# RMSNorm with doubled rows: squares by the whole tile, issued one tile ahead on ScalarE, and nearly all the copies on ScalarE

**Chip, cores, metric.** One core of a Trainium2 chip. The metric is the device time of one execution in microseconds (us); the span of the profiled execution is about 2 us shorter. All runs quoted are at a granted clock of 1.0.

## The reference

```python
B, S, D = 8, 512, 2048                      # float32
x_rep  = np.repeat(x, 2, axis=1)            # each row twice
rms    = np.sqrt((x_rep ** 2).mean(axis=-1, keepdims=True) + 1e-6)
out    = (x_rep / rms) * gamma              # [8, 1024, 2048]
```

33.6 MB are read and 67.1 MB written.

## The kernel before

Eight tiles. A tile is 128 partitions by 4 rows of 2048; its buffer has 8 row slots. The load fills slots 4 to 7, the scaled rows go to slots 0, 2, 4, 6, their copies to 1, 3, 5, 7, and one store writes all eight. There are three buffers, so load i+3 waits until store i has landed. All loads and stores go through SyncE, in program order.

```python
def square(i, k):                           # ScalarE: row squares into PSUM, with their sum
    sq = junk.tile([P, D], f32, name="sq")
    nc.scalar.activation(out=sq[:], in_=ys[i][:, 4 + k, :], func=Act.Square, accum_out=ss[:])
    nc.scalar.activation(out=rms[:], in_=ss[:], func=Act.Sqrt, scale=inv_d, bias=eps_t[:])
    ...
def scale(i, k, rms):                       # VectorE
    nc.vector.reciprocal(out=rstd[:], in_=rms[:])
    nc.vector.scalar_tensor_tensor(out=ys[i][:, 2 * k, :], in0=ys[i][:, 4 + k, :], scalar=rstd[:],
                                   in1=gamma_b[:], op0=Alu.mult, op1=Alu.mult)
def compute(i):
    for k in range(4):
        scale(i, k, square(i, k))
    repeat(i, 0, 2, nc.scalar.copy)         # copies of rows 0, 1
    repeat(i, 2, 4, nc.vector.tensor_copy)  # copies of rows 2, 3
...
load(0), load(1), load(2)
loads_after = {2: (3, 4, 5), 4: (6, 7)}
for i in range(8):
    compute(i)
    store(i, 0, 4)
    for j in loads_after.get(i, ()):
        load(j, nc.sync)
```

(Slot numbers are written out here; tile declarations and the load of gamma are cut.)

## Time and profile before

| | before |
|---|---|
| time, median | 239.9 us (239.40 to 240.17, 5 runs) |
| span of the profile | 237.9 us |
| instructions | 287 |
| VectorE busy | 96.5 us |
| ScalarE busy | 101.0 us |
| SyncE's queue, share of 16 engines' span | 98.5% |

The last row is the one to start from: the queue moves data during nearly the whole span, while both compute engines rest for over half of it. The lines that show this stand in the prediction. A store may be issued at any moment before the transfers queued ahead of it are over, less the time that it takes to start; only after that does lateness cost time.

A transfer is cut into packets, which 16 DMA engines move side by side. The trace records each packet's start, length, size and queue, but not its engine; where the text speaks of one engine, packets were chained, each to the one that ended as it began.

### The profile page before, as it was taken

Reading aid. Unit: us, or ns where it says so; the run is one execution under the profiler, and the core shown is the slowest. Engines: PE = TensorE matmul, PEld = TensorE weight load, DVE = VectorE, ACT = ScalarE, POOL = GpSimd, SP = SyncE. Lnnn points to the kernel's source line nnn. Section 1 sums busy time; section 2 is a strip of 40 time slices with the busy share of each in tenths; the row PEclk is TensorE's granted clock in tenths of the full one; section 3 lists DMA queues with packets and bytes.
Section 4 is the critical chain, followed back from the end, with each engine's and each line's share of the span. In section 5 each row is a group of like instructions: output and inputs, shape, how many; then the busy total and the mean of one; then the engine's idle time right before and its main releaser. Section 6 shows DMA issues by size and latency. Waiting matters only on the chain.

```text
span 237.9 us, 287 instructions
## 1 busy us (share of the span) xinstructions
DVE 96.5 (41%) x73; ACT 101.0 (42%) x106; POOL 2.5 (1%) x5
## 2 busy tenths in 40 slices
DVE  0049999960000000059999960000199990000000
ACT  2697999900000000099999920000599960000000
POOL 0030000000000000000000000000000000000000
DMA  7999998989899998999998999989998989999994
GB/s 265 436 446 441 441 441 353 530 353 496 386 452 430 397 485 353 441 441 441 441 518 364 464 419 430 452 369 430 435 518 364 518 364 485 397 452 430 408 474 176
DMA packets 2464, 100.69 MB, mean 423 GB/s; under 512 B 279, under 2 KB 285, under 8 KB 286
## 3 DMA queue, kind: packets, MB, share of 16 engines
q1 hardware_dynamic: 2448, 100.66, 98.5%
q14 instruction: 2, 0.02, 0.0%
q10 hardware_dynamic: 14, 0.01, 0.0%
HBM read 33.56 MB, written 67.11 MB: 423 GB/s over the span
## 4 chain that ended last, share of the span: by engine, by line
DMA 58%; ACT 12%; DVE 9%; issue 1%; POOLq 1%; ACTq 1%; SPq 0%
DMA y<-in_x_dram 33%; DMA out_dram<-y 21%; ACT sq L64 8%; DVE y L74 7%; DMA gamma_b<-in_gamma_dram 4%; ACT y L81 3%; DVE y L81 2%; ACT rms L68 1%; POOLq L136 1%; ACTq L95 1%; DVE rstd L73 0%; POOLq L96 0%; SPq L56 0%
## 5 line engine op out<-in xcount | busy, mean ns | idle before, releaser
L64 ACT ACTIVATE sq<-y 128x2048 f32<-128x2048 f32 x32 | 59.7, 1865 | 87.8 <-DMA y<-in_x_dram 87.8
L74 DVE SCALAR_TENSOR_TENSOR y<-y,rstd,gamma_b 128x2048 f32<-128x2048 f32 x32 | 75.3, 2352 | 4.1 <-POOL gamma_b L96 3.0
L73 DVE RECIPROCAL rstd<-rms 128x1 f32<-128x1 f32 x32 | 5.0, 158 | 94.6 <-ACT rms L68 94.3
L81 ACT COPY y<-y 128x4096 f32<-128x4096 f32 x8 | 28.7, 3590 | 1.4 <-DVE y L74 1.4
L81 DVE COPY y<-y 128x4096 f32<-128x4096 f32 x8 | 18.3, 2294 | 0.3
L68 ACT ACTIVATE rms<-ss,eps_t 128x1 f32<-128x1 f32 x32 | 9.4, 295 | 1.0
L64 ACT ACTIVATION_READ_ACCUMULATOR sq<-y 128x1 f32 x32 | 6.0, 187 | 0.0
L64 ACT ACT_TABLE_LOAD x1 | 1.3, 1283 | 3.0 <-issue 3.0
L96 POOL PARTITION_BROADCAST gamma_b<-gamma_b x1 | 2.3, 2294 | 12.2 <-DMA y<-in_x_dram 12.2
L68 ACT ACT_TABLE_LOAD x1 | 1.3, 1283 | 0.0
L98 DVE MEMSET eps_t<- 128x1 f32 x1 | 0.1, 59 | 0.8 <-PEq L125 0.8
L125 POOL MEMSET const-uint8-127<- 128x1 uint8 x1 | 0.1, 102 | 0.0
L125 POOL MEMSET const-bfloat16-1.0<- 128x1 bf16 x1 | 0.1, 101 | 0.0
L125 POOL MEMSET const-float32-0.0<- 128x1 f32 x1 | 0.1, 98 | 0.2 <-issue 0.2
L125 POOL MEMSET const-float32-1.0<- 128x1 f32 x1 | 0.1, 98 | 0.0
## 6 DMA issues: line engine op xcount, KB each, us to landing
y<-in_x_dram SPq DMA_DIRECT2D x7, 4096.0 KB, 14.6
y<-in_x_dram SPq DMA_DIRECT2D x2, 2048.0 KB, 7.4
out_dram<-y SPq DMA_DIRECT2D x8, 24.4
gamma_b<-in_gamma_dram ACTq DMA_DIRECT2D x6, 1.0 KB
gamma_b<-in_gamma_dram ACTq DMA_DIRECT2D x1, 2.0 KB
```

Source lines behind the costliest of these rows:

```text
L64: nc.scalar.activation(out=sq[:], in_=ys[i][:, K * (R - 1) + k, :], func=Act.Square, accum_out=ss[:])
L68: nc.scalar.activation(out=rms[:], in_=ss[:], func=Act.Sqrt, scale=inv_d, bias=eps_t[:])
L73: nc.vector.reciprocal(out=rstd[:], in_=rms[:])
L74: nc.vector.scalar_tensor_tensor(out=ys[i][:, R * k, :], in0=ys[i][:, K * (R - 1) + k, :], scalar=rstd[:], in1=gamma_b[:], op0=Alu.mult, o ...
L81: copy(out=y_r[:, k0:k1, 1, :], in_=y_r[:, k0:k1, 0, :])
L95: nc.scalar.dma_start(out=gamma_b[0:1, c0:c1], in_=gamma[c0:c1].partition_broadcast(1))
L96: nc.gpsimd.partition_broadcast(out_ap=gamma_b[:], in_ap=gamma_b[0:1, :])
L98: nc.vector.memset(eps_t, eps)
L125: nc = _bacc.Bacc("TRN2", target_bir_lowering=False, num_devices=1)
L136: with _tile.TileContext(nc) as tc:
```

## The change

The intent is to spend fewer instructions. A tile's squares are made by one ScalarE instruction over 8192 elements instead of four with accumulators, written to the slots of the buffer that are still free, and summed by one VectorE reduce. The wide square of tile i+1 is issued ahead of tile i's copies. Tiles 2, 5, 6 and 7 do this; tiles 0 and 3 still work row by row, and tiles 1 and 4 half and half. The copies, except for half of those of tiles 0 and 3, go to ScalarE. Core of the diff:

```diff
+    def square(i, k0, k1):
+        nc.scalar.activation(out=ys[i][:, k0:k1, :], in_=ys[i][:, 4 + k0 : 4 + k1, :], func=Act.Square)
+    def reduce(i, k0, k1, ss):
+        nc.vector.tensor_reduce(out=ss[:, k0:k1], in_=ys[i][:, k0:k1, :], op=Alu.add, axis=X)
+    def wide_tile(i):                       # the wide square of i was issued earlier
+        reduce(i, 0, K, ss); rsqrt(0, K, ss, rstd); scale(i, 0, K, rstd)
-    for i in range(ntiles):
-        compute(i)
-        store(i, 0, K)
-        for j in loads_after.get(i, ()): load(j, nc.sync)
+    ... (tiles 0 to 4)
+    store(4, 0, K)
+    for j in (6, 7): load(j, nc.sync)
+    for i in (5, 6, 7):
+        wide_tile(i)
+        if i < ntiles - 1:
+            square(i + 1, 0, K)
+        repeat(i, 0, H)                     # both copies on ScalarE, behind the square of i+1
+        repeat(i, H, K)
         store(i, 0, K)
```

(Shortened: slots written out, the row and half versions and tiles 0 to 4 cut.)

More of the change, by code (lines that the diff above doesn't have):

```diff
@@ L59, in store, with total @@
         )
-    def square(i, k):
+    def total(i, k, ss):
         sq = junk.tile([P, D], f32, name="sq")
-        ss = small.tile([P, 1], f32, name="ss")
         nc.scalar.activation(
-            out=sq[:], in_=ys[i][:, K * (R - 1) + k, :], func=Act.Square, accum_out=ss[:]
+            out=sq[:], in_=ys[i][:, K * (R - 1) + k, :], func=Act.Square, accum_out=ss[:, k : k + 1]
         )
-        rms = small.tile([P, 1], f32, name="rms")
-        nc.scalar.activation(out=rms[:], in_=ss[:], func=Act.Sqrt, scale=inv_d, bias=eps_t[:])
-        return rms
@@ L71, in scale @@
-    def scale(i, k, rms):
-        rstd = small.tile([P, 1], f32, name="rstd")
-        nc.vector.reciprocal(out=rstd[:], in_=rms[:])
-        nc.vector.scalar_tensor_tensor(
-            out=ys[i][:, R * k, :], in0=ys[i][:, K * (R - 1) + k, :], scalar=rstd[:], in1=gamma_b[:],
-            op0=Alu.mult, op1=Alu.mult,
-        )
-    def repeat(i, k0, k1, copy):
+    def square(i, k0, k1):
+        x_at = K * (R - 1)
+        nc.scalar.activation(
+            out=ys[i][:, k0:k1, :], in_=ys[i][:, x_at + k0 : x_at + k1, :], func=Act.Square
+        )
@@ new lines, in reduce, with rsqrt, scale @@
+    def reduce(i, k0, k1, ss):
+        nc.vector.tensor_reduce(
+            out=ss[:, k0:k1], in_=ys[i][:, k0:k1, :], op=Alu.add, axis=mybir.AxisListType.X
+        )
+    def rsqrt(k0, k1, ss, rstd):
+        nc.scalar.activation(
+            out=rstd[:, k0:k1], in_=ss[:, k0:k1], func=Act.Sqrt, scale=inv_d, bias=eps_t[:]
+        )
+        nc.vector.reciprocal(out=rstd[:, k0:k1], in_=rstd[:, k0:k1])
+    def scale(i, k0, k1, rstd):
+        for k in range(k0, k1):
+            nc.vector.scalar_tensor_tensor(
+                out=ys[i][:, R * k, :], in0=ys[i][:, K * (R - 1) + k, :], scalar=rstd[:, k : k + 1],
+                in1=gamma_b[:], op0=Alu.mult, op1=Alu.mult,
+            )
@@ L80, in repeat, with columns, rows_tile @@
+    def repeat(i, k0, k1, copy=nc.scalar.copy):
         y_r = ys[i].rearrange("p (k r) d -> p k r d", r=R)
         copy(out=y_r[:, k0:k1, 1, :], in_=y_r[:, k0:k1, 0, :])
-    def compute(i):
-        for k in range(K):
-            scale(i, k, square(i, k))
-        repeat(i, 0, K // 2, nc.scalar.copy)
-        repeat(i, K // 2, K, nc.vector.tensor_copy)
+    H = K // 2
+    def columns():
+        return small.tile([P, K], f32, name="ss"), small.tile([P, K], f32, name="rstd")
+    def rows_tile(i, copy=nc.vector.tensor_copy):
+        ss, rstd = columns()
+        for k0 in (0, H):
+            for k in range(k0, k0 + H):
+                total(i, k, ss)
+            rsqrt(k0, k0 + H, ss, rstd)
+            scale(i, k0, k0 + H, rstd)
+        repeat(i, 0, H)
+        repeat(i, H, K, copy)
@@ L90, with half_tile @@
+    def half_tile(i):
+        ss, rstd = columns()
+        square(i, H, K)
+        for k in range(H):
+            total(i, k, ss)
+        reduce(i, H, K, ss)
+        rsqrt(0, K, ss, rstd)
+        scale(i, 0, K, rstd)
+    def wide_tile(i):
+        ss, rstd = columns()
+        reduce(i, 0, K, ss)
+        rsqrt(0, K, ss, rstd)
+        scale(i, 0, K, rstd)
     ctx.enter_context(tc.manual_schedule())
@@ L104 @@
     assert ntiles == 8
-    loads_after = {2: (3, 4, 5), 4: (6, 7)}
-    for i in range(ntiles):
-        compute(i)
+    rows_tile(0)
+    store(0, 0, K)
+    half_tile(1)
+    square(2, 0, K)
+    repeat(1, 0, H)
+    repeat(1, H, K)
+    store(1, 0, K)
+    wide_tile(2)
+    repeat(2, 0, H)
+    repeat(2, H, K)
+    store(2, 0, K)
+    for j in (3, 4, 5):
+        load(j, nc.sync)
+    rows_tile(3)
+    store(3, 0, K)
+    half_tile(4)
+    square(5, 0, K)
+    repeat(4, 0, H)
+    repeat(4, H, K)
+    store(4, 0, K)
+    for j in (6, 7):
+        load(j, nc.sync)
+    for i in (5, 6, 7):
+        wide_tile(i)
+        if i < ntiles - 1:
+            square(i + 1, 0, K)
+        repeat(i, 0, H)
+        repeat(i, H, K)
         store(i, 0, K)
-        for j in loads_after.get(i, ()):
-            load(j, nc.sync)
 _INS = ['x', 'gamma']
```

## The prediction

> **What bounds the kernel now.** I read the page first. The engines' busy rows, the DMA row and the queue table:
>
> ```profile
> DVE 96.5 (41%) x73; ACT 101.0 (42%) x106; POOL 2.5 (1%) x5
> DMA  7999998989899998999998999989998989999994
> q1 hardware_dynamic: 2448, 100.66, 98.5%
> ```
>
> One queue, SyncE's, moves 100.66 MB and its packets fill 98.5% of the span; VectorE and ScalarE work for 41% and 42% of it. So arithmetic costs time only where it leaves the queue empty. Whether it comes close to that is read from the order of issues on SyncE, in the timeline of that engine (start, length, one issue each; only the second half is needed here):
>
> ```profile
> 91.56 0.33 SPq L52 DMA_DIRECT2D y<-in_x_dram  x1
> 115.86 0.34 SPq L56 DMA_DIRECT2D out_dram<-y  x1
> 128.25 0.34 SPq L56 DMA_DIRECT2D out_dram<-y  x1
> 140.24 0.34 SPq L52 DMA_DIRECT2D y<-in_x_dram  x1
> 159.63 0.34 SPq L52 DMA_DIRECT2D y<-in_x_dram  x1
> 160.08 0.37 SPq L56 DMA_DIRECT2D out_dram<-y  x1
> 184.02 0.34 SPq L56 DMA_DIRECT2D out_dram<-y  x1
> 196.41 0.33 SPq L56 DMA_DIRECT2D out_dram<-y  x1
> ```
>
> These are load 5, stores 3 and 4, loads 6 and 7, stores 5, 6 and 7. The packet records of the trace say when each actually moved: load 5 until 120.6 us, store 3 until 140.2, store 4 until 159.6, load 6 until 169.3, load 7 until 179.3 (its first engine is through at 177.9), then stores 5, 6, 7 back to back until 237.3. A store takes 19.3 us (8 packets of 2.42 us on each engine), a load 9.7 us. There is no gap anywhere after about 3 us: total bytes set the end. Each store therefore has a deadline, the end of what is queued ahead of it, less the start-up of a transfer. Store 5 was issued 19 us before its own. The start-up is seen once on an empty queue: the first load is issued at 0.72 and its packets start between 2.23 and 3.01 us, so 1.5 to 2.3 us.
>
> The chain and ScalarE's timeline show what compute waits for in the last third:
>
> ```profile
> 140.24 29.08 DMA y<-in_x_dram
> 169.32 0.02 issue
> ...
> 169.34 1.88 ACT L64 ACTIVATE sq<-y 128x2048 f32<-128x2048 f32 x1 [30.91 <-DMA y<-in_x_dram]
> ```
>
> Load 6 is issued at 140.24, because its buffer is free only when store 3 has landed, and it lands at 169.3. ScalarE's first square of tile 6 sits 30.91 us waiting for it. That idles nothing that matters today, because tile 5 has been finished since about 140.6 us and its store needs only SyncE.
>
> **What the skill says.** "ScalarE: Activation LUTs", section What ACT_TABLE_LOAD costs: an activation with immediate operands takes 186 ns plus 0.833 ns for each element of a row, and neighbours overlap by some 93 ns. The trace agrees: 3590 ns for the copy of 4096 (3413 + 177), and 3.49 us from its start to that of the next instruction. "VectorE: DVE Perf Modes", section The perf-mode tier table: tensor_reduce has only the 1x mode. This trace has no reduce, so its time is an estimate from that: one element a cycle at 0.96 GHz, 8.53 us for 8192 elements, plus the fixed 0.16 us that the trace's copy has over its 2.13 us. "DMA: Bandwidth & Descriptors", section Anatomy of one DMA: a semaphore wait happens on the issuing sequencer, before dispatch, and the DMA engines just consume their queues. The issue times above agree: the queue runs dry if SyncE is kept waiting. "SBUF — State Buffer", section SBUF: two separate sides: engine and DMA ports cannot contend. The trace agrees: 426 GB/s at 120-140 us, with both engines over 90% busy, and 423 at 200-220 us with both idle; so I charge nothing for the squares that now go to SBUF.
>
> **The change part by part.** Bytes, queue and order of SyncE's issues are unchanged (I compared the instruction orders of both builds). What moves is when each store is ready.
>
> Costs. A wide square: 8192 x 0.833 + 0.18 = 7.0 us, start to next start 6.9; a half one 3.6. 20 of the 32 row squares go (12 stay: 4 each in tiles 0 and 3, 2 each in tiles 1 and 4), 20 x (1.865 + 0.187) = 41.0 us with their accumulator reads, and come back as 4 x 7.0 + 2 x 3.6 = 35.2 us. ScalarE gains six copies of VectorE (6 x 3.59 = 21.5 us) and loses 22 of 32 Sqrt (22 x 0.29 = 6.4). ScalarE: 101.0 - 41.0 + 35.2 + 21.5 - 6.4 = about 110 us. VectorE gains reduces, 4 x 8.7 + 2 x 4.4 = 43.6 us, loses six copies (6 x 2.29 = 13.7) and 22 reciprocals (3.5): about 123 us. Both are half the span still. None of this is on the path by itself.
>
> The path: the new order on ScalarE for tiles 5, 6, 7 is Sqrt of tile i, wide square of tile i+1, then the two copies of tile i. So tile 5's copies stand behind a square that needs load 6. That turns ScalarE's harmless wait into one in front of store 5.
>
> I walked the stores through with these durations (us, before / after / deadline; deadline = end of the transfer ahead, its first engine, less 2.3):
> - Store 0: 27.05 / 26.9 / 30.6. Gamma still releases the first scale at 14.9; one reciprocal a pair is saved.
> - Store 1: 39.2 / 45.9 / 49.9. Half square until 26.9, reduce until 31.3, four scales until 41.3, copies behind the wide square of tile 2: 38.6 + 3.5 + 3.6 (the second one waits for the last scale).
> - Store 2: 51.4 / 63.7 / 69.3. Reduce 41.3 to 50.0, scales to 60.1, last copy to 63.7.
> - Store 3: 115.86 / 117.75 / 117.6. Load 3 lands at 101.2 as before; the first scale waits for two squares and a Sqrt (105.75 instead of 103.74). Just in time.
> - Store 4: 128.25 / 136.5 / 136.9. Half square 114.0-117.6, reduce to 122.1, Sqrt, wide square of tile 5 122.4-129.3, two copies. Just in time.
> - Store 5: 160.08 / **183.4** / 175.6. Its scales are over at about 151, but the square of tile 6 starts at 169.34; + 6.93 (to the next start) + 3.49 + 3.59 = 183.35, and 0.06 to the issue. **Late.**
> - Store 6: 184.0 / 199.4 / 202: reduce 176.3-185.0, square of tile 7 185.3-192.3, copies behind it. In time behind the late store 5.
> - Store 7: 196.4 / 217.5 / 221. In time.
>
> So one gap opens. Load 7 ends at 179.3 on its slowest engine; store 5 is issued at 183.4 and its packets start 1.5 to 2.3 us later, on the slowest engine at about 185.7. 185.7 - 179.3 = 6.4 us, less up to 0.8 if a store starts faster than the first load, plus up to 0.3 for a slow first packet and some tenths if store 3 or 4 misses its deadline. I take +6.3. Three stores follow it seamlessly, so nothing gives it back: span 237.9 + 6.3 = 244.2, time 239.9 + 6.3 = 246.2 us, 2.6% longer.
>
> **The rivals.** (a) Nothing changes: the queue is the bound at 98.5% and compute has over half its time free. For it: no bytes change, and all stores but one keep their deadline. Against: the order on ScalarE, which is fixed by the program, and the 30.91 us wait in front of tile 6's square. It would need the copies of tile 5 to come before that wait; they do not. Time 239.5 to 240.5. (b) Slower still: the reduce becomes the bound, if it costs twice the estimate (17 us for a wide tile). Then store 4 would be issued near 141, about 3 us late, and tiles 6 and 7 would run 17 + 9.4 us of VectorE each, against 19.3 us for a store, so that stores 6 and 7 come late too (store 7 near 233): some 257 us. Against it: the scale of 2048 elements takes 2352 ns with two inputs, already near one element a cycle, and a reduce has no reason to be slower. (c) Fewer instructions and no waits for rows make it faster: impossible by more than a few tenths, since the bytes take 234 of the 237.9 us. (d) Stores 3 and 4 miss too, each by up to 1 us: 247 to 248.
>
> **Range and chances.** The large terms (169.3, 6.9, 7.1, 179.3) are read from the trace; open are the start-up (0.8), the deadlines of stores 3 and 4 (0 to 1), and the scatter of a run (239.46 to 239.91). So 246.2, with 245.0 to 247.5 for 8 in 10. The line of 2% is at 244.7, 1.5 us below my number: slower 0.88, within 2% 0.11, faster 0.01.
>
> **What would show it.** Right: the wide square of tile 6 starts at about 169.3 and ends at 176.3; the fourth from last issue of the queue (load 7) stays at 159.6 and the next, store 5, is at 183.4; the DMA row shows one lowered slice at 178 to 186 us, and full ones elsewhere; the chain at the end runs store, ScalarE copy, wide square, load 6. Store 3 near 117.8 and store 4 near 136.5. Wrong: a lowered slice near 120 or 140 (deadlines of stores 3 and 4), a reduce far from 8.7 us, a square far from 7.0, or a start-up of the store well under 1.5 us, which takes a little from the sum.

## The result, and the profile after

246.48 us (246.21 to 246.80, 5 runs) against 239.9 (5 runs): ratio 1.0279, 95% interval 1.0263 to 1.0295, 2.8% slower. A ratio here and below is the mean time of one kernel's fast runs over that of the other kernel's fast runs of the same rounds, so it is not quite the ratio of the medians quoted.

The page of the changed kernel, its busy and DMA rows and its queue:

```profile
DVE 123.5 (50%) x51; ACT 113.7 (46%) x56; POOL 2.5 (1%) x5
DMA  7999999797979899999989797999909797989894
q1 hardware_dynamic: 2448, 100.66, 95.9%
```

Bytes are the same, the queue's share has fallen from 98.5 to 95.9%, and one of the 40 slices (6.1 us each) is empty. Stretches of time with the busy time of VectorE, ScalarE and GpSimd, then clock, DMA share and GB/s, put the hole to the microsecond (a packet is counted where it starts, so that a share can exceed 1):

```profile
170.00:178.00 8.00, 1.48 (x1) 8.00 (x2) 0.00 (x0) 1.00 0.92 394
178.00:184.00 6.00, 6.00 (x1) 5.49 (x2) 0.00 (x0) 1.00 0.00 0
184.00:186.00 2.00, 1.60 (x3) 0.76 (x2) 0.00 (x0) 1.00 1.23 524
```

No packet starts between 178 and 184 us. Both engines work in that hole; at what, the timeline shows (start, length, engine, line, and in brackets the idle time before it and what ended it):

```profile
140.97 9.27 DVE L87 SCALAR_TENSOR_TENSOR y<-y,rstd,gamma_b 128x2048 f32<-128x2048 f32 x4
169.46 7.03 ACT L70 ACTIVATE y<-y 128x8192 f32<-128x8192 f32 x1 [28.74 <-DMA y<-in_x_dram]
176.39 7.09 ACT L94 COPY y<-y 128x4096 f32<-128x4096 f32 x2
176.52 8.69 DVE L75 TENSOR_REDUCE ss<-y 128x4 f32<-128x8192 f32 x1 [26.29 <-ACT y L70]
```

And SyncE's issues of load 7 and store 5:

```profile
159.59 0.34 SPq L52 DMA_DIRECT2D y<-in_x_dram  x1
183.51 0.34 SPq L56 DMA_DIRECT2D out_dram<-y  x1
```

Tile 5 is scaled by 150.2 us. Its copies wait in ScalarE's program order behind the square of tile 6, which waits 28.74 us for load 6. They end at 183.5, store 5 is issued at 183.51 (160.08 before), and load 7 was through by then. By the packet records, load 7 ends on its 16 engines between 177.58 and 178.35 us, and store 5's packets start between 184.36 and 184.50.

One remark on clocks. When I wrote the prediction I had laid the packet records 0.5 us too late against the instructions. Ends of transfers and start-ups shift together, so its differences stand; from here on the records are aligned by the instructions, and ends are 0.5 us lower than those it names.

The chain that ended last, as the pages print it, before and after, needs care here:

```profile
DMA 58%; ACT 12%; DVE 9%; issue 1%; POOLq 1%; ACTq 1%; SPq 0%
DMA 40%; DVE 37%; ACT 8%; issue 1%; POOLq 1%; ACTq 1%; SPq 0%
```

VectorE's 37% against 9% before looks like a new bound. It is not: the chain is followed from the last store to whatever released its issue, and store 7 was issued at 217.15, when store 5 was through and store 6 still had 7 us to run. The wait that ends last for the last bytes is their place in the queue. In such a kernel, compare issue times with the ends of transfers, whatever the chain names.

### The profile page after: what moved, and what is told of

The parts are those of the page before. It is cut to its first block, busy times and chain, and to the rows that moved or that the text cites. A ratio compares the mean times of both kernels' runs of the same rounds, so it can differ in the third digit from the quotient of the medians.

```text
span 244.7 us, 219 instructions
## 1 busy us (share of the span) xinstructions
DVE 123.5 (50%) x51; ACT 113.7 (46%) x56; POOL 2.5 (1%) x5
## 3 DMA queue, kind: packets, MB, share of 16 engines
q1 hardware_dynamic: 2448, 100.66, 95.9%
## 4 chain that ended last, share of the span: by engine, by line
DMA 40%; DVE 37%; ACT 8%; issue 1%; POOLq 1%; ACTq 1%; SPq 0%
DMA y<-in_x_dram 27%; DVE y L87 22%; DVE ss L75 12%; DMA out_dram<-y 9%; DMA gamma_b<-in_gamma_dram 4%; ACT y L94 3%; ACT y L70 3%; DVE y L94 2%; ACT sq L63 2%; POOLq L198 1%; ACTq L134 1%; ACT rstd L80 1%; DVE rstd L83 0%; SPq L56 0%; POOLq L135 0%
## 5 line engine op out<-in xcount | busy, mean ns | idle before, releaser
L87 DVE SCALAR_TENSOR_TENSOR y<-y,rstd,gamma_b 128x2048 f32<-128x2048 f32 x32 | 74.0, 2350 | 1.5 <-POOL gamma_b L135 0.9
L75 DVE TENSOR_REDUCE ss<-y 128x4 f32<-128x8192 f32 (+1 forms) x6 | 43.6, 7261 | 26.3 <-ACT y L70 26.3
L94 ACT COPY y<-y 128x4096 f32<-128x4096 f32 x14 | 50.0, 3598 | 14.0 <-DVE y L87 14.0
L70 ACT ACTIVATE y<-y 128x8192 f32<-128x8192 f32 (+1 forms) x6 | 35.3, 5885 | 30.7 <-DMA y<-in_x_dram 30.7
L63 ACT ACTIVATE sq<-y 128x2048 f32<-128x2048 f32 x12 | 22.5, 1875 | 42.0 <-DMA y<-in_x_dram 41.8
L83 DVE RECIPROCAL rstd<-rstd 128x4 f32<-128x4 f32 (+1 forms) x10 | 1.7, 171 | 61.2 <-ACT rstd L80 61.2
L80 ACT ACTIVATE rstd<-ss,eps_t 128x4 f32<-128x4 f32 (+1 forms) x10 | 3.0, 297 | 13.7 <-DVE ss L75 13.6
L94 DVE COPY y<-y 128x4096 f32<-128x4096 f32 x2 | 4.6, 2294 | 0.1
L63 ACT ACTIVATION_READ_ACCUMULATOR sq<-y 128x1 f32 x12 | 2.2, 187 | 0.0
```

The costliest lines, as they stand in the source:

```text
L63: nc.scalar.activation(out=sq[:], in_=ys[i][:, K * (R - 1) + k, :], func=Act.Square, accum_out=ss[:, k : k + 1])
L70: nc.scalar.activation(out=ys[i][:, k0:k1, :], in_=ys[i][:, x_at + k0 : x_at + k1, :], func=Act.Square)
L75: nc.vector.tensor_reduce(out=ss[:, k0:k1], in_=ys[i][:, k0:k1, :], op=Alu.add, axis=mybir.AxisListType.X)
L80: nc.scalar.activation(out=rstd[:, k0:k1], in_=ss[:, k0:k1], func=Act.Sqrt, scale=inv_d, bias=eps_t[:])
L83: nc.vector.reciprocal(out=rstd[:, k0:k1], in_=rstd[:, k0:k1])
L87: nc.vector.scalar_tensor_tensor(out=ys[i][:, R * k, :], in0=ys[i][:, K * (R - 1) + k, :], scalar=rstd[:, k : k + 1], in1=gamma_b[:], op0= ...
```

## The experiments

Ten runs of nine kernels (run 10 repeats run 5), of three to five rounds each; all gave correct results. Runs 1 to 4 shared one chip, 5 to 8 another, 9 and 10 a third, each with the kernel before in the same rounds.

**1. The order alone.** In the changed kernel the copies of tile 5 go before the wide square of tile 6; the rest is untouched.

```diff
     wide_tile(i)
-    if i < ntiles - 1:
-        square(i + 1, 0, K)
+    if i == 6:
+        square(7, 0, K)
     repeat(i, 0, H)
     repeat(i, H, K)
+    if i == 5:
+        square(6, 0, K)
     store(i, 0, K)
```

> The changed kernel with one order altered: tile 5's two copies stand before the wide square of tile 6. Theory A (the order alone opens the gap, and all else costs nothing) expects 239.9 us. Theory B, which I hold after reading the changed trace: store 5 is on time (issue near 155), but tile 6 still takes 30 us from landing to issue (169.5 to 199.5), which the late store 5 had hidden; store 6 then starts near 201.0 where store 5 ends at 198.6, so a gap of 2.4 us opens there, and the time is 242.3. Rival R1 (the wide reduces and squares themselves, or their writes to SBUF, slow the transfers): stays near 246.5.

Measured: 242.63 us (242.61 to 242.80), 1.0128 of the kernel before (1.0113 to 1.0143). Against the kernel before in the same rounds (239.52) the loss is 3.1 us where it was 6.6, so 3.5 us are back, not all. Its DMA row has lost the empty slice and has a lowered one later, near 200 us:

```profile
DMA  7999998989898989999989898989999968989894
```

Its timelines show tile 6 from its square to the issue of store 6:

```profile
169.18 7.03 ACT L70 ACTIVATE y<-y 128x8192 f32<-128x8192 f32 x1 [15.42 <-DMA y<-in_x_dram]
184.96 0.30 ACT L80 ACTIVATE rstd<-ss,eps_t 128x4 f32<-128x4 f32 x1 [8.75 <-DVE ss L75]
192.08 7.09 ACT L94 COPY y<-y 128x4096 f32<-128x4096 f32 x2
...
199.20 0.34 SPq L56 DMA_DIRECT2D out_dram<-y  x1
```

Square, reduce, scales and copies take 30.0 us from the square's start to the issue; the row version before took 14.7 (169.34 to 184.02). Store 5 now ends between 197.18 and 198.40, and store 6's packets start at 200.04 to 200.19. In the changed kernel this second lateness was hidden behind the first: store 5 ran until 203.9 there, and store 6, issued at 199.48, was in time. Theory A falls and B holds. R1 falls too: the same wide instructions are all still there, and over half of the loss is gone. That the time lies so near B's 242.3 is partly luck: on the slowest engines the gap is 1.8 us (198.40 to 200.19), not 2.4, and an instruction fetch at 210.11 us then held up one engine for about 0.9 us, as one did in the changed kernel (see below).

**2. One copy of the two.** As 1, but only tile 5's first copy goes ahead.

```diff
     wide_tile(i)
+    if i == 5:
+        repeat(5, 0, H)
     if i < ntiles - 1:
         square(i + 1, 0, K)
-    repeat(i, 0, H)
+    if i != 5:
+        repeat(i, 0, H)
     repeat(i, H, K)
```

> Only the first of tile 5's two copies goes before the wide square. Store 5 is then issued at 169.46 + 6.93 + 3.60 = 180.0 and starts at 181.5 (2.2 to 2.5 late). Store 6 stays at 199.5, start 201.0, where store 5 ends at 200.9. Theory B: 242.3 to 242.6, hardly different from the run with both copies first. Theory A: 239.9 + 2.5 = 242.4 here too, but then 239.9 for the run with both. R1: 246.5.

Measured: 242.67 us (242.52 to 242.77), the same as 1. Store 5 was issued at 179.43 and its packets started at 180.27, against load 7's end at 178.06; it ended at 199.83 at the latest, and store 6 (issued 198.90, packets from 199.77) just caught it. Two late stores do not add: the later of the two decides.

**3 and 4. The old kernel, with only the order.** No wide square, no reduce. Tile 5's ScalarE copy and its store are moved into tile 6, behind its fourth (run 3) or its first (run 4) row square.

```diff
     def compute(i):
         for k in range(K):
             scale(i, k, square(i, k))
-        repeat(i, 0, K // 2, nc.scalar.copy)
+            if i == 6 and k == 3:           # run 4: k == 0
+                repeat(5, 0, K // 2, nc.scalar.copy)
+                store(5, 0, K)
+        if i != 5:
+            repeat(i, 0, K // 2, nc.scalar.copy)
         repeat(i, K // 2, K, nc.vector.tensor_copy)
```

> The kernel before, with no wide square and no reduce; only tile 5's ScalarE copy is moved behind the four row squares of tile 6. The copy runs 178.2 to 181.8, store 5 is issued at 181.9 and starts at 183.4, where load 7 ended at 179.3: order theory 244.0 to 244.6. R1, and the theory that the wide instructions matter: 239.9.

> The same, with the copy behind only the first row square of tile 6: copy 171.6 to 175.1, store 5 issued at 175.2, start 176.7, before the queue's first engine runs dry at 177.9. Deadline theory: 239.9, although store 5 is issued 15 us later than before. A theory in which each us that a store is issued later costs time expects 240.5 or more.

Measured: behind four 243.90 us (243.87 to 243.91), 1.0179 (1.0162 to 1.0196), a tenth below the range named; behind one 239.43 us (239.36 to 239.59), 0.9993 (0.9979 to 1.0008). The issue of store 5, behind four and behind one:

```profile
181.76 0.34 SPq L56 DMA_DIRECT2D out_dram<-y  x1
```

```profile
175.00 0.34 SPq L56 DMA_DIRECT2D out_dram<-y  x1
```

In run 3 the packets start at 182.60 to 182.75, with load 7 ended by 178.56: a gap of 4.2 us on the slowest engine, and a time longer by 4.4. In run 4 store 5 is issued 15 us later than in the kernel before and costs nothing, as its engines are busy with load 7 until 177.41 at least. This is the deadline, from both sides and without any new instruction.

**5. Repair both.** Tile 5's copies first, and tile 6 row by row as tiles 0 and 3 are. Three wide squares of four remain.

```diff
-    for i in (5, 6, 7): ...
+    wide_tile(5); repeat(5, 0, H); repeat(5, H, K); store(5, 0, K)
+    rows_tile(6); store(6, 0, K)
+    square(7, 0, K)
+    wide_tile(7); repeat(7, 0, H); repeat(7, H, K); store(7, 0, K)
```

> Tile 5's copies first, and tile 6 squared row by row (as tiles 0 and 3 are) instead of wide; tiles 2, 5 and 7 stay wide, and 1 and 4 half and half. Store 6 should be issued near 186 and store 7 near 211, both in time. Theory B: 239.9 (within 0.4). R1 (wide squares, reduces or SBUF writes cost as such, three of four wide squares are still here): above 243.

Measured: 240.72 us (239.93 to 240.77), 1.0027 (1.0001 to 1.0053): a miss of my 0.4 us, though far from 243. Store 6 was issued at 185.66, store 7 at 211.52, both in time, and no gap opened. So the three wide squares that are left, the reduces and the writes to SBUF cost at most this remainder; what that is, runs 9 and 10 ask.

**6 and 7. The same extra work in two places.** Run 5's kernel, with four row squares of gamma, whose result is thrown away, in front of tile 5's copies (run 6) or tile 4's (run 7).

```diff
+    def busy():
+        for _ in range(4):
+            sq = junk.tile([P, D], f32, name="sq")
+            nc.scalar.activation(out=sq[:], in_=gamma_b[:], func=Act.Square)
...
     wide_tile(5)
+    busy()                                  # run 6
     repeat(5, 0, H)
...
     square(5, 0, K)
+    busy()                                  # run 7
     repeat(4, 0, H)
```

> As the run before, with four more row squares (of gamma, result thrown away, about 7.5 us of ScalarE) in front of tile 5's copies. They delay store 5 from about 155 to about 156, far from its deadline of 176. Expected: no cost, 239.9 (within 0.4). A theory of ScalarE's load would have 7 us more.

> The same 7.5 us of ScalarE in front of tile 4's copies. Store 4 was issued at 136.2 with store 3 ending at 139.9 and 1.5 us of start-up, so it has some 2 us to spare: issue near 143.7, start near 145.3, gap 5.4 us, and all later loads and stores move with it: 245.3 (244.8 to 245.9).

Measured: 240.26 us (239.85 to 240.81) for run 6, which is run 5's time within its scatter; 246.72 us (246.55 to 246.88) for run 7, 1.0287 (1.0270 to 1.0305). In run 7 the timeline has the work and the issue where I expected them:

```profile
129.20 7.60 ACT L125 ACTIVATE sq<-gamma_b 128x2048 f32<-128x2048 f32 x4
136.74 7.09 ACT L94 COPY y<-y 128x4096 f32<-128x4096 f32 x2
...
143.85 0.34 SPq L56 DMA_DIRECT2D out_dram<-y  x1
```

The gap is as expected too, from store 3's end at 139.60 to store 4's packets at 144.85 on the slowest engines: 5.25 us. The time is 1.4 us over my sum. The packets account for it: on the slowest engines store 4 starts 5.10 us later than in the kernel before (139.75 to 144.85), but the last packet ends 7.06 us later (236.76 to 243.82). In between, store 4 took 20.36 us instead of 19.3 and load 7 10.84 instead of 9.7, both in their last packets, where a transfer of the other direction followed. Why these turns cost up to 1.1 us in some runs is not settled. What the pair does show is that 7.6 us of ScalarE are worth nothing in one place and over 5 us in another.

**8. Let load 6 land sooner.** The changed kernel with its order kept, but load 6 is issued on ScalarE's queue, so that it may share the engines with store 4.

```diff
-    for j in (6, 7): load(j, nc.sync)
     for i in (5, 6, 7):
         wide_tile(i)
+        if i == 5:
+            load(6, nc.scalar); load(7, nc.sync)
         if i < ntiles - 1:
             square(i + 1, 0, K)
```

> The changed kernel, order of ScalarE's compute kept; load 6 is issued from ScalarE's queue at about 141 instead of SyncE's, so that it can run beside store 4 and land sooner. Store 5 follows load 6's landing L by 14.05 us (6.93 + 3.5 + 3.6): if L is near 160, store 5 comes near 174, in time, and tile 6 too: 239.9 to 240.5. If the two queues alternate packet by packet, load 6's 32 KB against store 4's 64 KB, L is near 169 as before and the time 246.5. Between them it should follow L + 14.05 + 1.5 for store 5's start.

Measured: 246.45 us (246.01 to 248.19), 1.0290 (1.0249 to 1.0331), the same as the changed kernel. The profiled execution is the slowest of the four, at 248.19 us. Load 6 did not land sooner in it:

```profile
140.68 0.36 ACTq L52 DMA_DIRECT2D y<-in_x_dram  x1
171.19 7.03 ACT L70 ACTIVATE y<-y 128x8192 f32<-128x8192 f32 x1 [30.21 <-DMA y<-in_x_dram]
...
185.24 0.33 SPq L56 DMA_DIRECT2D out_dram<-y  x1
```

Its packets began at 146.19, 5.5 us after its issue, behind three packets of store 4 on fifteen engines and four on one, and then took turns with those of store 4, one of 32 KB after one of 64 KB, every 3.63 us. Store 5 followed the square's start by 14.05 us to the hundredth. So this run confirms the sum from the landing of load 6 to store 5, but as a remedy it does nothing.

**9 and 10. The remainder of run 5.** Run 10 is run 5's kernel again, five rounds. Run 9 is the same with fourteen of the throw-away squares in front of tile 5's copies.

```diff
     def busy():
-        for _ in range(4):
+        for _ in range(14):
...
     wide_tile(5)
+    busy()
     repeat(5, 0, H)
```

> The repaired kernel (tile 6 by rows, tile 5's copies first) came out 0.3 to 1.1 us over the kernel before, and its packets where load 7 turns into store 5 took up to 1.1 us too long; where store 5 was issued at 175.0 instead of 160 they did not. So here fourteen throw-away row squares (about 26.5 us) hold tile 5's copies until store 5 is issued near 174.3, still before its deadline of 176. If a store that stands early behind a load costs at the turn: 239.5, 0.7 us less than the same kernel without the squares, with 26 us more work. If it is mere scatter between builds: the same as the other, 240.2 to 240.7. A deadline missed by a little: 240.5 and over, with a gap in the packets at 178.

> The repaired kernel without the throw-away squares, again, to be compared with the run above on one chip: 240.2 to 240.7 if its small excess is real, 239.9 if it was scatter.

Measured on one chip: run 10 240.53 us (240.30 to 240.69), 1.0032 (1.0020 to 1.0044); run 9 240.06 us (239.87 to 240.59), 1.0017 (1.0005 to 1.0029). The excess of run 5 is real and small, 0.7 us by the medians. Run 9's store 5 was issued at 174.37, and the 26 us of added work gave about half of the excess back by the ratios, where I had asked for all; but its packets at the turn from load 7 to store 5 were still up to 0.75 us too long, which the theory of the early store had ruled out. That theory falls as I put it. Run 9 was not quite clean either: its store 7 was issued only at 216.56, with the first engine through at 216.28, and its packets started at 217.39 to 217.54; by the packets this cost under 0.1 us, as one engine was busy until 217.53. In the kernel before the same turn costs under 0.3 us.

The packet records show where else to look. Ahead of the turn from store 4 to load 6, the last packets of store 4 reached 2.8 to 3.2 us on a few engines in the changed kernel and in runs 1, 2, 5, 6, 9 and 10, but at most 2.5 (2.42 is usual) in the kernel before and in runs 3 and 4. So slow turns there go with the wide version, whenever its store 5 is issued, and in the changed kernel both compute engines rest at that time (155 to 159 us), so that work running beside the transfer is not the cause there. Yet the kernel before has a slow turn of its own, from load 2 to store 0 (10.2 to 11.0 us instead of 9.7). What makes a turn slow, and with it this remainder, stays open. No version beats the kernel before, and by the bytes none could by much.

## Why the prediction was right

- **The bound, and the place of the loss.** Right. One gap, in front of store 5, made by ScalarE's order; runs 1 to 4 show it with and without the wide instructions. That the queue runs dry while SyncE waits, which the prediction read from the issue times of the kernel before, could not be seen there, as that queue never ran dry; the changed kernel shows it, with no packet between 178.35 and 184.36. A slip besides: "19 us before its own" counts to the end of load 7. By the prediction's own deadline of 175.6 store 5 had 15.5 us to spare.
- **The durations.** Wide square 7.03 us (7.0 predicted), reduce of 8192 8.68 to 8.69 (8.7), half reduce 4.42 (4.4), ScalarE 113.7 us in all (about 110; the sum took the lengths of the single instructions and left out that neighbours overlap) and VectorE 123.5 (about 123).
- **The walk of the stores.** Issues of stores 0 to 7: predicted 26.9, 45.9, 63.7, 117.75, 136.5, 183.4, 199.4, 217.5; measured 26.69, 47.47, 63.06, 117.52, 136.23, 183.51, 199.48, 217.15. Only store 1 is off by more than 0.7 us: I let the wide square of tile 2 start at 31.6, but it waited 1.97 us for load 2, until 33.41. This is the same trap as at tile 6, at a place where it was still in time.
- **"Just in time" at stores 3 and 4.** They were better off. A store's start-up on an empty queue was 0.85 us to its first and 0.99 to its last engine, where the first load, which I had used, has 1.0 to 1.8 on the aligned clock. No gap opened at either.
- **The sum.** The time is longer by 6.58 us, 6.3 was predicted. Two terms were off and nearly cancelled, which is luck. With the faster start-up, store 5 starts 5.69 us later than before on the slowest engine (178.81 to 184.50), not 6.4. And "three stores follow it seamlessly" left something out: an instruction fetch of 8 KB at 208.95 us fell between two packets of one engine, which took 2.71 and 2.78 us instead of 2.42 with 0.30 us between them. One engine ended store 6 at 224.10, the other fifteen by 223.31. From store 5's start to the end, 58.9 us passed instead of 57.95. Together 5.69 + 0.97 = 6.66, and the profiled ends are 236.76 and 243.42.
- **What would show it.** Of its signs of being right all came but one: I expected the chain at the end to run through the wide square and load 6. As shown above, it went through VectorE's work on tile 7. Of its signs of being wrong one came, the store's start-up well under 1.5 us (0.85), and it took 0.7 us from the sum, as it said.
- **Rival (a)**, nothing changes, falls with the time itself. **Rival (b)**, a reduce twice as dear, falls with its 8.68 us. **(c)** and **(d)** did not come about.
- **What the prediction did not see** is what run 1 found: moving the copies would not have been enough, since tile 6 itself takes 30 us from landing to store and would have been late by about 2 us (198.40 to 200.19 on the slowest engines).

## What to carry to other kernels

When transfers fill the span, write down for each store when it is ready and when the queue ahead of it runs dry; busy shares say nothing of that, and an engine at half load can still open the one gap that counts. Putting the next tile's work ahead of this tile's last step puts the next tile's load in front of this tile's store on an engine that works in order. After one late store is repaired, look for the next one that it had hidden.

## What the Trainium skill lacked or had wrong

- "DMA: Bandwidth & Descriptors", Specifications: it gives about 0.6 us to the first byte for DMAs from the sync and scalar queues. It does not say from when that counts. Here a store of 8.4 MB on an idle queue took 0.83 to 0.85 us from the start of its issue to its first packet (the changed kernel and runs 1, 2, 3, 7, 8), which is 0.5 us from the end of the 0.34 us issue; the first load took 1.0 us from the start.
- "DMA: Bandwidth & Descriptors", Queues, rings and completion order: its turn by turn service between queues at packet granularity is what run 8 shows (32 KB and 64 KB packets alternating every 3.63 us). It does not say how long a transfer on the second queue may wait for its first turn: load 6's first packet came 5.5 us after its issue, behind three or four packets of store 4. Why is not shown.
- Neither the same page nor any other that I read has what it costs where a load and a store follow each other on one queue: the last packets ahead of the turn from load 7 to store 5 took 0 (run 4) to 1.1 us (run 5) longer.
- "Runtime: NRT & Kernel Launch", Instruction fetch mechanics, has the fetches, but not what one costs the data: here 8 KB held up one DMA engine by about 0.9 us at 209 us, and the slowest engine sets the end.
- "VectorE: DVE Perf Modes", The perf-mode tier table, has no duration for tensor_reduce: 8.68 us for 128x8192 and 4.42 us for 128x4096 in fp32, which is its 1x mode with 0.15 us on top.
